# No arithmetic on GpSimd, and a residual summed by accumulating DMAs

## The chip, the cores and the metric

The kernel runs on one core of one Trainium2 chip. The metric is the device time of one execution in microseconds (us). The core's engines run side by side, each through its own queue in order, and wait for each other by semaphores: TensorE (PE in the profile; its weight loads are PEld), VectorE (DVE), ScalarE (ACT), GpSimd (POOL) and SyncE (SP), which only issues DMAs.

## The reference

One sequence of 512 positions with 1024 features goes through two parts, all in float32.

The first part is two layers. Each projects x into three kinds of attention (six heads dilated, four differential, six latent) and joins them; then, with alpha = 4 to the power of 1/4:

```python
h = layer_norm(DEEPNORM_ALPHA * x + heads @ w_o, ln1_g, ln1_b)
ffn = (jax.nn.silu(h @ w_gate) * (h @ w_up)) @ w_down
return layer_norm(DEEPNORM_ALPHA * h + ffn, ln2_g, ln2_b)
```

The second part is one block with modulation vectors (from `w_mod`): a feed-forward part over the sequence and over 256 context positions; then a mixer: retention in both directions over four heads, a convolution of 31 taps over each channel with a layer norm behind it, and two gates:

```python
return (jax.nn.sigmoid(ga) * y_ret + jax.nn.sigmoid(gb) * y_conv) @ w_o
```

and a last feed-forward part with an RMS norm.

## The kernel before

All tensors lie transposed: a tile is 128 features by 512 positions, eight of them (m = 0 to 7) make one state. Every matrix product is taken in three: a float32 operand is split into a high part in the rounded format that TensorE reads, and a low part that is the rest, and high·high, high·low and low·high are summed in PSUM (`mm3`, lines 141 to 145).

**Weights.** `wload` (line 111) loads 512 KB `raw` by SyncE, ScalarE casts it to `whi` (line 109), and `wlo = raw - whi` is a subtraction (line 110) on VectorE or on GpSimd, as `self.wpool` says: it is (0,) (VectorE) nearly everywhere, (1,) for the 16 gate weights of the mixer, and (1, 0), every other one on GpSimd, from there to the mixer's end. Three buffers hold split weights; `hold(2)` adds two.

**Stage ends.** The output projection, the feed-forward parts and the mixer make eight output tiles. The first three go over all 512 positions; the other five (`HELD`) first over positions 0 to 255 for all five, then over 256 to 511, so that the norm of the first half runs on the other engines while TensorE does the second. `ln_add` collects, per tile, the sum `accd` (line 202) and with `sq_add` the sum of squares `accq` (line 216); `ln_first` (line 183) takes K, the feature mean of the first tile, from that tile, and the other tiles get K taken off too. In the feed-forward ends of the two layers these sums run on GpSimd for m below 7 (`"pool": "dq"`, and `"q"` for the RMS norm after the second). `ln_stats` makes mean and variance with TensorE and a short chain of tiny VectorE instructions; `ln_apply` and `affine` write the normed tile as high (`uh`) and low (`ul`) part, and every third low part is taken by GpSimd (line 270).

**Output projection.** `out_chunk` (line 435) multiplies `w_o` with the heads `H` and adds the PSUM result to `D[m]`. `D[m]` is prepared before by two VectorE instructions: `rt` = alpha·xh − K and `D` = alpha·xl + `rt`, where xh and xl are the high and low part of x. PSUM has three buffers `mm` for such products; a buffer is free once the addition has read it.

**Attention.** Eight units in the order `UNITS` = a0 a1 c0 c1 b0 c2 b1 a2; the projections of later units are filled in between the softmax work of earlier ones, so x is read by TensorE until the last unit's projections are done. GpSimd starts DMAs here: the bias tables `T` and the stacked operands `st`.

**Mixer.** `conv_step` hands out taps (line 1147, one `cz` per tap) a few at a time between projections; what is left runs at the end. Then the transposed retention output is normed and gated (`gtd`, line 1262), written to DRAM and read back; `gates` computes 16 gate tiles, nine before and seven after the layer norm statistics of the convolution.

The order on each engine is made by a planner: it takes instructions in program order as priority, and starts each when its inputs are ready by its own estimate of times. So an instruction can stand ahead of one that was written earlier.

Of the kernel before, what the change touches and what calls it, by code (L numbers as in the profile page):

```python
# [9 lines left out]
F32 = mybir.dt.float32  # L10
# [52 lines left out]
class Kern:  # L63
    def __init__(self, ctx, tc, a, o):
# [21 lines left out]
        self.whx = None  # L86
        self.nw = 0

        self.wpool = (0,)
        self.turn = 0  # L90
# [15 lines left out]

    def split(self, src, hi, lo, pool=False):
        nc = self.nc
        nc.scalar.copy(hi, src)  # L109
        (nc.gpsimd if pool else nc.vector).tensor_tensor(out=lo, in0=src, in1=hi.bitcast(F32), op=ALU.subtract)  # L110

    def wload(self, src, key=None):
        if key in self.pre:
            return self.pre.pop(key)
        n = src.shape[-1]
        raw = self.wraw.tile([128, 1024], F32, tag="raw", name="raw")[:, :n]
        self.nc.sync.dma_start(out=raw, in_=src)
        p = self.whl
        if self.whx is not None:
            if self.turn % (3 + self.nx) >= 3:  # L120
                p = self.whx
            self.turn += 1
        hi = p.tile([128, 1024], F32R, tag="hi", name="whi")[:, :n]
        lo = p.tile([128, 1024], F32R, tag="lo", name="wlo")[:, :n]
        self.nw += 1
        self.split(raw, hi, lo, self.wpool[self.nw % len(self.wpool)])
        return hi, lo
# [64 lines left out]
    def ln_add(self, st, m, D, sl=FULL):  # L192
        nc, tmp = self.nc, self.tmp
        if m == 0:
            self.ln_first(st, D)
            st["D0"] = D
        self.sq_add(st, m, D, self.tmp, sl)
        if m == 1:
            st["accd"] = tmp.tile([128, 512], F32, tag="accd", name="accd", bufs=1)
        if m > 0:  # L200
            e = nc.gpsimd if m < 7 and "d" in st.get("pool", "") else nc.vector
            e.tensor_tensor(out=st["accd"][:, sl], in0=(st["D0"] if m == 1 else st["accd"])[:, sl], in1=D[:, sl], op=ALU.add)

    def sq_add(self, st, m, D, p, sl=FULL):
        nc = self.nc
        n = D.shape[-1]
        sl = slice(sl.start, min(sl.stop, n))
        sq = p.tile([128, n], F32, tag="sq", name="sq", bufs=2)
        nc.scalar.activation(out=sq[:, sl], in_=D[:, sl], func=AF.Square)
        if m == 0:  # L210
            st["sq0"] = sq
        else:
            if "accq" not in st:
                st["accq"] = p.tile([128, n], F32, tag="accq", name="accq", bufs=1)
            e = nc.gpsimd if m < 7 and "q" in st.get("pool", "") else nc.vector
            e.tensor_tensor(out=st["accq"][:, sl], in0=(st["sq0"] if m == 1 else st["accq"])[:, sl], in1=sq[:, sl], op=ALU.add)

# [42 lines left out]
    def affine(self, t, g, b, y, x, func=AF.Identity, sl=FULL):  # L260
        nc = self.nc
        nc.scalar.activation(out=y, in_=t, func=func, scale=g, bias=b)
        if x is not None:
# [5 lines left out]
            self.nlo += 1  # L269
            (nc.vector if self.nlo % 3 else nc.gpsimd).tensor_tensor(out=lo, in0=y, in1=hi.bitcast(F32), op=ALU.subtract)  # L270

# [137 lines left out]
    def layer(self, l, X):  # L409
# [5 lines left out]
        with ExitStack() as st:  # L415
            pool = lambda name, bufs: st.enter_context(tc.tile_pool(reuse_waits=RW, name=f"{name}{l}", bufs=bufs))
            self.kq, self.lat, self.pp, self.pt, self.T = pool("kq", 2), pool("lat", 1), pool("pp", 3), pool("pt", 2), pool("T", 2)
            self.tables(self.lat)
            self.wpool = (0,)
            self.attention(l, X, H, lam_init, hp)  # L420
# [9 lines left out]
        stt = {}  # L430
        self.wpool = (0,)
        order = (0, 5, 1, 6, 3, 7, 4, 2)
        stt3 = nc.vector.scalar_tensor_tensor

        def out_chunk(m, sl):
            ps = self.ps_mm.tile([128, 512], F32, tag="mm", name="mm")[:, sl]
            self.chunk(ps, W[m], H, order=order, sl=sl)
            nc.vector.tensor_tensor(out=D[m][:, sl], in0=D[m][:, sl], in1=ps, op=ALU.add)
            self.ln_add(stt, m, D[m], sl)

        for m in range(8):
            xh, xl = (t.bitcast(F32) for t in X[m])
            t = self.tmp.tile([128, 512], F32, tag="t", name="rt")
            if m > 0:
                stt3(out=t, in0=xh, scalar=ALPHA, in1=stt["K"], op0=ALU.mult, op1=ALU.subtract)
            else:
                nc.vector.tensor_scalar(out=t, in0=xh, scalar1=ALPHA, scalar2=None, op0=ALU.mult)
            D.append(accp.tile([128, 512], F32, tag=f"h{m}", name=f"D{m}"))
            stt3(out=D[m], in0=xl, scalar=ALPHA, in1=t, op0=ALU.mult, op1=ALU.add)
            W.append(self.wload(a["w_o"][l, m]))  # L450
            if m < 8 - HELD:
                out_chunk(m, FULL)
# [11 lines left out]

        self.wpool = (0,)
        with ExitStack() as st:
# [4 lines left out]
            acc = [accp.tile([128, 512], F32, tag=f"h{m}", name=f"acc{m}") for m in range(8)]  # L471
            stt = {"pool": "dq"}

# [22 lines left out]
            U = []  # L496
            st2 = {"pool": "q"}

# [121 lines left out]
    def attention(self, l, X, H, lam_init, hp):  # L620
# [237 lines left out]
        for n in range(2 * len(units) + 1):  # L858
            i, hh = n // 2, n % 2
            head = None  # L860
            if i < len(units):
                if hh == 0:
# [3 lines left out]
                    while len(ready) <= i:  # L866
                        step()
                    unit = i
                    maps, *rest = att[units[i][0]](units[i][1], *ready[i])
# [117 lines left out]
    def block2(self, h, X):  # L987
# [46 lines left out]
        st3 = {}  # L1034
        self.wpool = (0,)

# [253 lines left out]
    def mix_out(self, U, h, g2, stt2, tail):  # L1290
        nc, a, tc, tmp = self.nc, self.a, self.tc, self.tmp
        with ExitStack() as st:
# [9 lines left out]

            self.wpool = (1,)
            gates(0, GATES_FIRST)
# [11 lines left out]
            gates(GATES_FIRST, 16)  # L1316
            self.wpool = (1, 0)
            Y = self.mod_tiles()
# [189 lines left out]
```

## Time and profile before

| | |
|---|---|
| time, median of 3 runs | 3099.66 us (3099.3 to 3102.32) |
| profiled execution | 3099.42 us |
| its span, first to last instruction | 3097.6 us |
| mean granted TensorE clock | 0.991 of 2.4 GHz |
| TensorE busy | 3024.2 us (98%) |
| VectorE busy | 1880.2 us (61%), 3552 instructions |
| ScalarE busy | 1158.2 us (37%) |
| GpSimd busy | 275.2 us (9%), 318 instructions |

Busy time is time in which an engine executes. An engine that isn't busy waits, and the profile names what ended the wait, the releaser. The granted clock is given in parts of 2.4 GHz, so 0.50 is 1.2 GHz.

### The profile page before, as it was taken

The page shows a single profiled execution, that of the slowest core. Times are in us where ns is not written, and L with a number is a line of the kernel's source. Part 1 is how long each engine was busy: PE and PEld are TensorE (multiplying, and loading weights), DVE is VectorE, ACT ScalarE, POOL GpSimd, SP SyncE. Part 2 cuts the span into 40 slices and gives each one's busy share as a digit, 9 for nine tenths or more (in the row PEclk, how much of TensorE's full clock was granted, in tenths as well). Part 3 has the DMA queues.
Part 4 walks back from the last instruction along what each step waited for, and adds up shares of the span by engine and source line. Part 5 has one row for each costly group of instructions (what it writes and reads, how often), then busy time and mean ns, then how long its engine had stood idle before and what let it go on. Part 6 is the DMA issues. An engine that isn't in the chain of part 4 may idle for free.

```text
span 3097.6 us, 40929 instructions
## 1 busy us (share of the span) xinstructions
PE 3024.2 (98%) x15961; PEld 2566.7 (83%) x15961; DVE 1880.2 (61%) x3552; ACT 1158.2 (37%) x1908; POOL 275.2 (9%) x318
## 2 busy tenths in 40 slices
PE   9998999999999999999999999999999999999998
PEld 6778888887779888898888888988888778888887
DVE  5988657576888554473323238587887555553334
ACT  4874322245765222262121227433223253342222
POOL 0110000030210000130000001100000343100000
PEclk9999999999999999999999999999999999999999
DMA  4332445322323554322212125623223324233331
GB/s 136 86 86 82 163 136 191 127 85 75 99 85 109 163 170 132 100 93 86 74 53 70 55 69 191 212 83 119 99 92 99 112 86 153 93 103 95 95 94 63
DMA packets 103649, 334.07 MB, mean 108 GB/s; under 512 B 13164, under 2 KB 16364, under 8 KB 103328
## 3 DMA queue, kind: packets, MB, share of 16 engines
q1 hardware_dynamic: 89232, 289.83, 29.5%
q0 software_dynamic: 13136, 40.59, 4.3%
q8 instruction: 125, 2.05, 0.3%
q10 hardware_dynamic: 1088, 1.05, 0.1%
q14 instruction: 68, 0.56, 0.1%
HBM read 312.51 MB, written 14.71 MB: 106 GB/s over the span
## 4 chain that ended last, share of the span: by engine, by line
PE 73%; issue 14%; DVE 7%; ACT 5%; POOL 1%; DMA 1%; POOLq 0%; SPq 0%; DVEq 0%; ACTq 0%
PE mm L143 20%; PE mm L144 20%; PE mm L145 20%; DVE cz L1147 1%; PE gc L145 1%; PE gc L143 1%; PE gc L144 1%; PE pvps L374 1%; ACT P L330 1%; DVE wlo L110 1%; ACT whi L109 1%; PE tps L358 1%; PE dc L145 1%; PE dc L144 1%; PE dc L143 1%
## 5 line engine op out<-in xcount | busy, mean ns | idle before, releaser
L109 ACT CAST whi<-raw 128x1024 fp32r<-128x1024 f32 (+3 forms) x524 | 505.7, 966 | 1402.3 <-PE mm L144 1160.5
L144 PE MATMUL mm<-ul,whi 128*128 128x512 f32 (+2 forms) x2288 | 864.3, 379 | 2.2 <-POOL ul L270 1.7
L143 PE MATMUL mm<-uh,whi 128*128 128x512 f32 (+2 forms) x2288 | 862.9, 380 | 0.8 <-ACT cl L644 0.3
L145 PE MATMUL mm<-uh,wlo 128*128 128x512 f32 (+2 forms) x2288 | 861.9, 378 | 0.3 <-DVE wlo L110 0.2
L110 DVE TENSOR_TENSOR wlo<-raw,whi 128x1024 fp32r<-128x1024 f32 (+3 forms) x484 | 549.4, 1136 | 388.1 <-ACT whi L109 378.7
L144 PEld LDWEIGHTS mm<-ul,whi 128*128 128x128 f32 (+1 forms) x2288 | 431.9, 189 | 82.7 <-POOL ul L270 3.3
L145 PEld LDWEIGHTS mm<-uh,wlo 128*128 128x128 f32 (+1 forms) x2288 | 431.4, 189 | 82.1 <-DVE wlo L110 0.8
L143 PEld LDWEIGHTS mm<-uh,whi 128*128 128x128 f32 (+1 forms) x2288 | 429.8, 189 | 81.0 <-ACT uh L266 1.3
L143 PE MATMUL mm<-hh,whi 128*128 128x512 f32 (+1 forms) x789 | 292.6, 371 | 1.4 <-DVE acc L482 0.7
L144 PE MATMUL mm<-hl,whi 128*128 128x512 f32 (+1 forms) x789 | 292.3, 370 | 0.0
L145 PE MATMUL mm<-hh,wlo 128*128 128x512 f32 (+1 forms) x789 | 291.7, 370 | 0.3 <-DVE wlo L110 0.3
L527 DVE TENSOR_TENSOR g<-g,mm 128x512 f32<-128x512 f32 (+1 forms) x96 | 61.7, 643 | 277.1 <-PE mm L145 273.7
L1147 DVE SCALAR_TENSOR_TENSOR cz<-cy,vec,cz 128x512 f32<-128x512 f32 x240 | 179.2, 773 | 2.2
L143 PEld LDWEIGHTS mm<-hh,whi 128*128 128x128 f32 x789 | 150.3, 191 | 27.0 <-issue 1.1
L145 PEld LDWEIGHTS mm<-hh,wlo 128*128 128x128 f32 x789 | 150.0, 190 | 26.7 <-DVE wlo L110 0.7
L144 PEld LDWEIGHTS mm<-hl,whi 128*128 128x128 f32 x789 | 150.1, 190 | 24.7 <-issue 0.2
L985 DVE SCALAR_TENSOR_TENSOR acc<-mm,g,acc 128x512 f32<-128x512 f32 (+1 forms) x61 | 43.1, 707 | 146.8 <-PE mm L145 146.7
L110 POOL TENSOR_TENSOR wlo<-raw,whi 128x1024 fp32r<-128x1024 f32 (+1 forms) x40 | 88.8, 2221 | 205.5 <-ACT whi L109 204.2
L145 PE MATMUL gc<-uch,wlo 128*128 128x256 f32 x352 | 98.8, 281 | 0.2 <-DVE wlo L110 0.2
L143 PE MATMUL gc<-uch,whi 128*128 128x256 f32 x352 | 98.6, 280 | 0.0
L144 PE MATMUL gc<-ucl,whi 128*128 128x256 f32 x352 | 98.4, 280 | 0.0
L330 ACT ACTIVATE P<-P,nm 128x128 f32<-128x128 f32 (+3 forms) x160 | 88.1, 553 | 20.9 <-DVE nm L326 20.5
(397 smaller groups left out, 4970.7 us busy)
## 6 DMA issues: line engine op xcount, KB each, us to landing
mr<-w_mod SPq DMA_DIRECT2D x72, 512.0 KB, 3.7
raw<-w_f1i SPq DMA_DIRECT2D x54, 512.0 KB, 3.5
raw<-w_gate SPq DMA_DIRECT2D x44, 512.0 KB, 3.6
raw<-w_up SPq DMA_DIRECT2D x44, 512.0 KB, 3.5
raw<-w_f2i SPq DMA_DIRECT2D x44, 512.0 KB, 3.5
raw<-w_in SPq DMA_DIRECT2D x36, 512.0 KB, 3.8
raw<-w_v SPq DMA_DIRECT2D x32, 512.0 KB, 4.0
raw<-w_qk SPq DMA_DIRECT2D x24, 512.0 KB, 3.5
```

The costliest lines, as they stand in the source:

```text
L109: nc.scalar.copy(hi, src)
L110: (nc.gpsimd if pool else nc.vector).tensor_tensor(out=lo, in0=src, in1=hi.bitcast(F32), op=ALU.subtract)
L143: mm(out=ps, lhsT=w[0], rhs=x[0], start=first, stop=False)
L144: mm(out=ps, lhsT=w[0], rhs=x[1], start=False, stop=False)
L145: self.last_mm = mm(out=ps, lhsT=w[1], rhs=x[0], start=False, stop=last)
L330: nc.scalar.activation(out=sl, in_=sl, func=AF.Exp, scale=scale, bias=nm[:, qb:qb + 1], accum_out=sm[:, qb:qb + 1])
L358: nc.tensor.transpose(out=ps[:, w:w + 128], in_=Pt[:, OFF[qb] + kb * 128:OFF[qb] + kb * 128 + 128], identity=self.ident)
L374: nc.tensor.matmul(out=out[:, kb * 128:512], lhsT=v, rhs=blocks[kb][part], start=i == 0, stop=i == 7)
L527: gm = nc.vector.tensor_tensor(out=g, in0=g, in1=pu, op=ALU.mult)
L985: self.nc.vector.scalar_tensor_tensor(out=h, in0=ps, scalar=g[:, m:m + 1], in1=h, op0=ALU.mult, op1=ALU.add)
L1147: nc.vector.scalar_tensor_tensor(out=z, in0=y[:, t:t + 512], scalar=w, in1=z, op0=ALU.mult, op1=ALU.add)
```

## The change

It has two parts.

First, every subtraction and sum that ran on GpSimd runs on VectorE: the weight splits of the mixer, the sums `accd` and `accq`, and the low parts in `affine`. GpSimd then only issues DMAs (and sets up a few constants at the start).

Second, in the output projection. When the last attention unit (number 7) begins in the program, eight DMAs on GpSimd's queue add xh onto xl in place, so that the tile xl holds x. `rt` and the old `D` are gone; `out_chunk` makes `D` = alpha·x + PSUM in one instruction, and for m above 0 takes K off in another.

```diff
-        (nc.gpsimd if pool else nc.vector).tensor_tensor(out=lo, in0=src, in1=hi.bitcast(F32), op=ALU.subtract)
+        nc.vector.tensor_tensor(out=lo, in0=src, in1=hi.bitcast(F32), op=ALU.subtract)
...
-            e = nc.gpsimd if m < 7 and "d" in st.get("pool", "") else nc.vector
-            e.tensor_tensor(out=st["accd"][:, sl], ...
+            nc.vector.tensor_tensor(out=st["accd"][:, sl], ...
...
-            e = nc.gpsimd if m < 7 and "q" in st.get("pool", "") else nc.vector
-            e.tensor_tensor(out=st["accq"][:, sl], ...
+            nc.vector.tensor_tensor(out=st["accq"][:, sl], ...
...
-            (nc.vector if self.nlo % 3 else nc.gpsimd).tensor_tensor(out=lo, in0=y, in1=hi.bitcast(F32), op=ALU.subtract)
+            nc.vector.tensor_tensor(out=lo, in0=y, in1=hi.bitcast(F32), op=ALU.subtract)
...
         def out_chunk(m, sl):
...
-            nc.vector.tensor_tensor(out=D[m][:, sl], in0=D[m][:, sl], in1=ps, op=ALU.add)
+            stt3(out=D[m][:, sl], in0=X[m][1].bitcast(F32)[:, sl], scalar=ALPHA, in1=ps, op0=ALU.mult, op1=ALU.add)
+            if m > 0:
+                nc.vector.tensor_tensor(out=D[m][:, sl], in0=D[m][:, sl], in1=stt["K"][:, sl], op=ALU.subtract)
             self.ln_add(stt, m, D[m], sl)
         for m in range(8):
-            xh, xl = (t.bitcast(F32) for t in X[m])
-            t = self.tmp.tile([128, 512], F32, tag="t", name="rt")
-            if m > 0:
-                stt3(out=t, in0=xh, scalar=ALPHA, in1=stt["K"], op0=ALU.mult, op1=ALU.subtract)
-            else:
-                nc.vector.tensor_scalar(out=t, in0=xh, scalar1=ALPHA, scalar2=None, op0=ALU.mult)
             D.append(accp.tile([128, 512], F32, tag=f"h{m}", name=f"D{m}"))
-            stt3(out=D[m], in0=xl, scalar=ALPHA, in1=t, op0=ALU.mult, op1=ALU.add)
...
+                    if i == 7:
+                        for xh, xl in X:
+                            nc.gpsimd.dma_start(out=xl.bitcast(F32), in_=xh.bitcast(F32), accum_op=ALU.add)
...
-            self.wpool = (1,)
             gates(0, GATES_FIRST)
...
             gates(GATES_FIRST, 16)
-            self.wpool = (1, 0)
```

## Rows read from the trace of the kernel before

**Rows 1.** The page: busy us, share of the span and instructions of each engine.
```profile
PE 3024.2 (98%) x15961; PEld 2566.7 (83%) x15961; DVE 1880.2 (61%) x3552; ACT 1158.2 (37%) x1908; POOL 275.2 (9%) x318
```
**Rows 2.** TensorE's waits: waiting, releaser, us in total, times, longest.
```profile
PE mm L143 <- DVE D L438: 12.2, 4, 4.6
PE gt L1260 <- DVE gtd L1262: 6.5, 1, 6.5
...
PE stps L226 <- DVE accd L202: 5.7, 3, 2.7
```
**Rows 3.** Windows: from:to, length, busy us (instructions) by engine, clock, DMA share.
```profile
core 0: us, PE busy (x) PEld busy (x) DVE busy (x) ACT busy (x) POOL busy (x), PEclk, DMA share, GB/s
248.00:272.00 24.00, 17.10 (x123) 16.65 (x121) 19.58 (x37) 4.83 (x9) 0.00 (x0) 0.86 0.20 66
914.00:938.00 24.00, 18.68 (x130) 18.22 (x128) 22.11 (x44) 7.17 (x16) 0.00 (x0) 0.86 0.22 66
636.00:664.00 28.00, 24.30 (x173) 23.06 (x171) 23.79 (x45) 7.64 (x13) 20.45 (x16) 0.94 0.24 78
1304.00:1328.00 24.00, 21.25 (x144) 19.80 (x143) 17.53 (x39) 6.50 (x11) 13.96 (x14) 0.93 0.18 62
...
2424.00:2446.00 22.00, 15.50 (x67) 12.60 (x66) 20.65 (x24) 3.19 (x5) 9.18 (x9) 0.84 0.39 139
2498.00:2516.00 18.00, 16.00 (x79) 13.14 (x78) 13.15 (x31) 6.76 (x10) 11.91 (x3) 0.91 0.18 59
```
**Rows 4.** VectorE's timeline: start, us, line, operation, tiles, count, [idle before, releaser].
```profile
634.97 1.29 DVE L481 TENSOR_TENSOR acc<-acc,lnk 128x512 f32<-128x512 f32 x2
...
642.33 1.77 DVE L481 TENSOR_TENSOR acc<-acc,lnk 128x512 f32<-128x512 f32 x1
...
653.81 0.93 DVE L202 TENSOR_TENSOR accd<-accd,acc 128x256 f32<-128x256 f32 x1 [2.40 <-POOL accd L202]
...
2397.67 2.72 DVE L1147 SCALAR_TENSOR_TENSOR cz<-cy,vec,cz 128x512 f32<-128x512 f32 x4
...
2423.51 12.88 DVE L1147 SCALAR_TENSOR_TENSOR cz<-cy,vec,cz 128x512 f32<-128x512 f32 x12
```
**Rows 5.** GpSimd's timeline: a table load of the attention, and weight splits.
```profile
208.22 0.55 POOL L306 DMA_DIRECT2D T<-brow  x1 [11.35 <-DVE mx L322]
...
2424.54 2.63 POOL L110 TENSOR_TENSOR wlo<-raw,whi 128x1024 fp32r<-128x1024 f32 x1 [2.60 <-ACT whi L109]
...
2498.74 11.36 POOL L110 TENSOR_TENSOR wlo<-raw,whi 128x1024 fp32r<-128x1024 f32 x2 [6.39 <-ACT whi L109]
```
**Rows 6.** Groups by line and form: busy us, mean ns | idle before, releasers.
```profile
L110 POOL TENSOR_TENSOR wlo<-raw,whi 128x1024 fp32r<-128x1024 f32 x24 | 66.4, 2770 | 158.3 <-ACT whi L109 158.2
...
L270 POOL TENSOR_TENSOR ul<-y,uh 128x256 fp32r<-128x256 f32 x16 | 11.8, 737 | 208.5 <-DVE uh L268 171.1 <-ACT uh L266 34.1 <-issue 3.4
...
L110 DVE TENSOR_TENSOR wlo<-raw,whi 128x1024 fp32r<-128x1024 f32 x366 | 450.1, 1231 | 306.1 <-ACT whi L109 296.6 <-PE mm L145 2.5
```
**Rows 7.** VectorE's timeline in the output projection of layer 0.
```profile
244.32 0.68 DVE L438 TENSOR_TENSOR D<-D,mm 128x512 f32<-128x512 f32 x1
...
249.02 1.29 DVE L445 SCALAR_TENSOR_TENSOR rt<-xh,lnk 128x512 f32<-128x512 f32 x2
...
259.84 1.30 DVE L449 SCALAR_TENSOR_TENSOR D<-xl,rt 128x512 f32<-128x512 f32 x2
...
262.18 0.76 DVE L438 TENSOR_TENSOR D<-D,mm 128x256 f32<-128x256 f32 x2
```
**Rows 8.** Instructions of line 449: ns min/median/max, first and last start.
```profile
L449 DVE SCALAR_TENSOR_TENSOR D<-xl,rt x8: 692/695/696, 238.7 to 260.4; 128x512 f32<-128x512 f32 x8
```
**Rows 9.** Window of the second half of the output projection, layer 0.
```profile
276.00:291.00 15.00, 14.85 (x122) 14.28 (x121) 14.67 (x45) 11.35 (x21) 1.48 (x2) 1.00 0.31 106
```
**Rows 10.** TensorE's timeline: the last product that reads x in layer 0.
```profile
213.53 0.39 PE L145 MATMUL mm<-xh,wlo 128*128 128x512 f32 x1
```
**Rows 11.** DMA issues: queue, count, KB each, median us to landing.
```profile
raw<-w_o SPq DMA_DIRECT2D x16, 512.0 KB, 4.1
...
T<-brow POOLq DMA_DIRECT2D x20, 256.0 KB, 3.6
```

More of the change, by code (lines that the diff above doesn't have):

```diff
@@ L86, in __init__ @@
         self.whx = None
-        self.nw = 0
-        self.wpool = (0,)
         self.turn = 0
@@ L104, in v, with split @@
         return self.vec[:, s:s + 1]
-    def split(self, src, hi, lo, pool=False):
+    def split(self, src, hi, lo):
         nc = self.nc
         nc.scalar.copy(hi, src)
-        (nc.gpsimd if pool else nc.vector).tensor_tensor(out=lo, in0=src, in1=hi.bitcast(F32), op=ALU.subtract)
+        nc.vector.tensor_tensor(out=lo, in0=src, in1=hi.bitcast(F32), op=ALU.subtract)
     def wload(self, src, key=None):
@@ L124, in wload @@
         lo = p.tile([128, 1024], F32R, tag="lo", name="wlo")[:, :n]
-        self.nw += 1
-        self.split(raw, hi, lo, self.wpool[self.nw % len(self.wpool)])
+        self.split(raw, hi, lo)
         return hi, lo
@@ L200, in ln_add @@
         if m > 0:
-            e = nc.gpsimd if m < 7 and "d" in st.get("pool", "") else nc.vector
-            e.tensor_tensor(out=st["accd"][:, sl], in0=(st["D0"] if m == 1 else st["accd"])[:, sl], in1=D[:, sl], op=ALU.add)
+            nc.vector.tensor_tensor(out=st["accd"][:, sl], in0=(st["D0"] if m == 1 else st["accd"])[:, sl], in1=D[:, sl], op=ALU.add)
     def sq_add(self, st, m, D, p, sl=FULL):
@@ L214, in sq_add @@
                 st["accq"] = p.tile([128, n], F32, tag="accq", name="accq", bufs=1)
-            e = nc.gpsimd if m < 7 and "q" in st.get("pool", "") else nc.vector
-            e.tensor_tensor(out=st["accq"][:, sl], in0=(st["sq0"] if m == 1 else st["accq"])[:, sl], in1=sq[:, sl], op=ALU.add)
+            nc.vector.tensor_tensor(out=st["accq"][:, sl], in0=(st["sq0"] if m == 1 else st["accq"])[:, sl], in1=sq[:, sl], op=ALU.add)
     def colsums(self, accs, eps):
@@ L418, in layer @@
             self.tables(self.lat)
-            self.wpool = (0,)
             self.attention(l, X, H, lam_init, hp)
@@ L430, in layer @@
         stt = {}
-        self.wpool = (0,)
         order = (0, 5, 1, 6, 3, 7, 4, 2)
@@ L463, in layer @@
             self.ctx_begin()
-        self.wpool = (0,)
         with ExitStack() as st:
@@ L471, in layer @@
             acc = [accp.tile([128, 512], F32, tag=f"h{m}", name=f"acc{m}") for m in range(8)]
-            stt = {"pool": "dq"}
+            stt = {}
             def down(pi, m, ps, pc, sl):
@@ L496, in layer @@
             U = []
-            st2 = {"pool": "q"}
+            st2 = {}
             def tail1(sl):
@@ L1034, in block2 @@
         st3 = {}
-        self.wpool = (0,)
         def down2(pi, m, ps, pc, sl):
```

## The prediction, made before the changed kernel was run

> **What bounds the kernel now.** I read the page's busy times first [rows 1]: TensorE is busy 98% of the span, VectorE 61%, GpSimd 9%. So the end is set by TensorE, and only two things can move it: time in which TensorE stands still, and time in which its granted clock is at the lower level. Then the list of TensorE's waits [rows 2]: its three largest entries are the places that the edits touch. 12.2 us go to VectorE's addition `D` of the output projection (line 438), 6.5 us to VectorE's `gtd` at the start of the mixer, 5.7 us to `accd`, the sum of the layer norm at the end of the feed-forward parts. Last the windows around these places [rows 3]: each says how long TensorE was idle (length less PE busy) and what clock it had (PEclk; 1.00 is 2.4 GHz, 0.50 is 1.2 GHz). After each stall the clock falls, so a stall costs twice. Idle time, and PE busy times (1 − PEclk):
>
> - output projection, layer 0: 6.9 and 2.4 us; layer 1: 5.3 and 2.6
> - end of the feed-forward part, layer 0: 3.7 and 1.5; layer 1: 2.8 and 1.5
> - start of the mixer: 6.5 and 2.5; its layer norm between the gates: 2.0 and 1.4
>
> That is 39 us, the most that the edits can win here. The reader is to see that VectorE is nearly full in each of these windows (19.6 of 24 us, 22.1 of 24, 20.7 of 22): TensorE waits for VectorE. What counts is whether the edits give VectorE more or less to do just there.
>
> **GpSimd slows VectorE.** The convolution taps show it [rows 4]. Four taps took 2.72 us at 2397, 0.68 each, with GpSimd idle; twelve took 12.88 us at 2423, 1.07 each, while GpSimd split weights (2.63 us the one at 2424) [rows 5]. The subtraction at line 481 takes 1.29 us for a pair at 635, 0.6 each, and 1.77 us alone at 642, under GpSimd's sums [rows 4]. The reverse holds too: two weight splits on GpSimd took 11.36 us together at 2498 [rows 5], against a mean of 2.77 [rows 6]. VectorE does a split in 1.23 us [rows 6], of which about 0.1 overlaps the next. So moving an instruction costs VectorE 1.14 us where it had been losing up to 2.4 us to the same work. Where VectorE was idle, the move costs it time that nobody waits for.
>
> **Output projection.** Removed are `rt` and the old `D` (lines 445 to 449), 8 and 8 per layer, 0.6 us in a row (1.29 for a pair [rows 7]) and 0.69 by itself [rows 8]. In layer 0 fourteen of them, 8.4 us, run between 249.0 and 261.1, and the addition that frees the PSUM buffer for TensorE comes only at 262.18, behind them [rows 7]; that is TensorE's largest stall. Added are subtractions of K: two whole (0.6) and ten half ones (0.33: a pair of half additions takes 0.76 [rows 7]), of which five lie in each half. The fused multiply-add replaces the old addition one for one and doesn't wait for K, so PSUM comes free sooner. In the first half VectorE gets 8.4 − 1.2 − 1.65 = 5.5 us back. What is late next is the second half, where VectorE also applies the layer norm: it is busy 14.67 of 15 us while TensorE, at full clock, is busy 14.85 [rows 9]. There it gets five subtractions (1.65 us) and some two or three of the moved low parts (0.33 each), 2.5 us, and TensorE waits for the last low part of the half. I take the first half's 5.5 us, part of the clock (2.4 us at most), less the 2.5: −4.5 us per layer, −9 for both. Ends: −17.2 (idle and clock all gone) and +5 (nothing won, 2.5 us late twice).
>
> **The accumulating DMAs.** Eight of 256 KB per layer, from GpSimd's queue, after the last read of x by TensorE (213.53 in layer 0 [rows 10]). The first sum is needed by `D` of m = 0, which ran at 244.32, and the last around 262 [rows 7]. Nothing of the attention is queued behind them in GpSimd's queue: its last table load was issued at 208 [rows 5]. No DMA of the trace accumulates. The nearest row is the table load of the same size and queue, 3.6 us to land [rows 11]: one after the other, eight would take 29 us and be there at 242 to 243. Overlapped, they take less; with read and write of the target, up to three times as long, 86 us. I take the row, cost 0, since the first has 31 us and the last 48. Lower end: 0, nothing waited for x before.
>
> **Feed-forward ends.** In the window of layer 0 GpSimd runs 16 sums, 20.5 us, in that of layer 1 14, 14.0 us [rows 3]. On VectorE they cost 0.6 us (whole) and 0.33 (half): 4 × 0.6 + 12 × 0.33 = 6.4 us and 4 × 0.6 + 10 × 0.33 = 5.7. In return the line 481 and the splits lose their stretching (1.77 against 0.6), some 4 us in either, and the 2.40 us that VectorE idled for GpSimd's last sum [rows 4] is time to work in. So VectorE ends about where it did, less that wait. I take −2.5 and −2, half of idle and clock: −4.5. Ends: −9.5 and +12 (no relief at all).
>
> **Mixer start.** 6.5 us of TensorE's wait is for `gtd`, ordered behind twelve taps that took 12.88 us instead of 8.2: 4.7 us late, and 1 or 2 us more on the instructions ahead. The stall is about this lateness. With the change two splits of 1.14 us stand there instead. The time thus falls by 6.2 − 2.3, about 4 us, and with most of the clock's 2.5: −6 us. Ends: −9 and +6 (the rival below).
>
> **Gates and layer norm of the convolution.** Three splits (3.4 us) come onto VectorE while it is full with the layer norm's subtractions and sums; against it stands the end of the two slow GpSimd splits. −1.5 us; ends −3.4 and +3.4. The other splits of the mixer run beside an idle VectorE, cost 0; were that cover gone, some 30 would cost 1.14 each.
>
> **Low parts of the normed tiles.** Two or three per half come from GpSimd (0.74 us [rows 6]) to VectorE (0.33 in a row), in about eight VectorE-paced halves, four outside the output projection: 4 × 2.7 × 0.33 = 3.6 us, against which GpSimd's slowness, a thing TensorE also waited for, ends. +1.5 us; ends 0 and +6.
>
> **Sum.** −9 − 4.5 − 6 − 1.5 + 1.5 = −19.5 us. The profiled execution took 3099.42 us, 1.8 more than its span, and lies 0.2 below the median of 3099.66; I set both equal: 3080 us.
>
> **Rivals.**
> 1. *VectorE becomes the bound (slower).* If GpSimd's work didn't stretch VectorE's as the taps suggest, every moved instruction would be added to a full engine: +12 (feed-forward ends), +3.4 (gates), +6 (low parts), +2.3 (mixer start), less 9 of the output projection, is +15: 3114 us. It decides itself at the feed-forward ends: slower if the added 6.4 and 5.7 us aren't outweighed by the shorter line 481. For it: these windows are full. Against it: 1.77 against 0.6 and 1.07 against 0.68. Chance 0.07.
> 2. *Splits queue behind the taps.* When TensorE comes to the first gate, about 20 taps (13 us at 0.66) and four `gtd` are left on VectorE. If the order puts them ahead of the splits, TensorE waits 6 us more than before instead of 6 less: 3092 us. For it: taps come earlier in the program. Against it: in the trace a split stands between taps wherever it was ready. Chance 0.12.
> 3. *Late sums of x.* At twice the table load's time the eighth sum lands 58 us after 213.5, at 271, 9 us after the need, in both layers: +18, 3098 us. It also covers weights held up: their loads take 4.1 us [rows 11]. Chance 0.08. The Trainium skill (DMA: Bandwidth & Descriptors, Issuing engines are not separate DMA queues) says that transfers started from any engine run on the same 16 DMA engines and interleave, so by it two loads of `w_o` that meet the sums take longer. By that rule, were both 4.1 us loads doubled on TensorE's path in both layers, the time would be 3080 + 16 = 3096. The trace shows a DMA share of 0.20 in that window [rows 3], which leaves room, so it gets no chance beyond the 0.08.
> 4. *More than forecast.* All idle and clock of the six windows gone but for 3 us of new waits: 3063 us. Chance 0.13: it needs an order that fits everywhere.
>
> **How the numbers follow.** The forecast has 0.60: 3080, own range 3068 to 3092. The range runs from 3062, below rival 4, to 3099, above rivals 2 and 3; rival 1 and the tails of 4 are left out. A measurement of this kernel can tell about 0.2%, 6 us, from no change. Faster than 3093.5: 0.60, 0.13, most of rival 2 and a little of 3, 0.83. Same: the rest of 2 and 3, 0.10. Slower: rival 1, 0.07.
>
> **What would show it.** Right: TensorE's waits for `D` (12.2), `gtd` (6.5) and `accd` (5.7) each below a half; taps at 0.66 throughout; line 481 at 0.6; no GpSimd arithmetic; all eight sums landed before `D` of m = 0. Wrong: TensorE waiting for the low part `ul`, for `wlo` at the first gates, or for a DMA on `xl`; the feed-forward windows longer than before.

## The result and the profile after

The changed kernel takes 3068.35 us (median of 4 runs, 3066.45 to 3070.85), the kernel before 3099.48 (median of 4, 3097.11 to 3102.32): a ratio of 0.9900 with a 95% interval of 0.9883 to 0.9917, 31 us less. The forecast was 3080, its own range 3068 to 3092. The sign, the places and the range held; the size came out at the lower edge, 1.6 times the forecast change, and two of the four runs lie below 3068.

The page of the kernel after has this line in place of [rows 1]:

```profile
PE 3012.2 (98%) x15961; PEld 2558.9 (84%) x15961; DVE 1894.4 (62%) x3673; ACT 1159.3 (38%) x1908; POOL 112.9 (4%) x205
```

The span fell from 3097.6 to 3064.4 us, by 33.2. TensorE's busy time fell by 12.0 us with the same 15961 products, which goes with the mean granted clock, 0.994 instead of 0.991. The other 21.2 us are time in which it stood still. VectorE's busy time grew by only 14.2 us, although 129 instructions came over from GpSimd.

TensorE's waits in the kernel after, answering [rows 2]; the columns are the same:

```profile
PE mm L139 <- DVE uh L262: 4.4, 7, 1.5
...
PE stps L220 <- DVE accd L197: 1.6, 2, 1.2
...
PE mm L140 <- DVE ul L264: 1.2, 5, 0.3
...
PE gt L1250 <- DVE gtd L1252: 0.3, 1, 0.3
...
PE mm L139 <- DVE D L431: 0.3, 1, 0.3
```

`D` went from 12.2 to 0.3 us, `gtd` from 6.5 to 0.3, `accd` from 5.7 to 1.6. Two waits for ScalarE now lead the list, 6.8 us for `Ph` in the attention and 6.2 for `xh` at the start; they were there before (6.8 and 6.0), and the change doesn't touch them. Behind them, and new, is `uh`, VectorE's cast of a normed tile, in small pieces.

Windows of the kernel after at the same places as [rows 3], shifted with the program, and two more (from 268 and from 1336); columns as there:

```profile
248.00:272.00 24.00, 23.99 (x203) 23.69 (x202) 21.70 (x59) 7.80 (x14) 0.00 (x0) 1.00 0.32 93
901.00:925.00 24.00, 23.53 (x199) 23.12 (x198) 22.56 (x65) 10.41 (x20) 0.00 (x0) 1.00 0.29 91
268.00:283.00 15.00, 13.52 (x102) 12.19 (x100) 14.69 (x46) 10.51 (x17) 0.00 (x0) 1.00 0.54 176
628.00:656.00 28.00, 27.26 (x213) 26.32 (x211) 26.58 (x72) 9.09 (x16) 0.00 (x0) 1.00 0.29 95
...
1285.00:1309.00 24.00, 24.00 (x184) 22.86 (x183) 22.41 (x60) 8.71 (x15) 0.00 (x0) 1.00 0.26 78
2397.00:2419.00 22.00, 21.68 (x104) 17.82 (x103) 21.86 (x35) 7.12 (x9) 5.25 (x10) 1.00 0.45 153
2469.00:2487.00 18.00, 17.91 (x89) 14.95 (x88) 14.70 (x34) 6.99 (x10) 1.07 (x2) 0.91 0.32 102
...
1336.00:1366.00 30.00, 26.83 (x202) 26.04 (x201) 25.59 (x78) 19.92 (x42) 0.00 (x0) 0.90 0.29 89
```

At the six places of [rows 3] TensorE is now busy for nearly the whole window, in five of them at full clock; at the gates (2469 to 2487) the idle time is gone, but the clock is still 0.91. The other two windows show a price. In the second half of the output projection (268 to 283) VectorE is as full as before [rows 9], and TensorE now stands still for 1.5 us. And from 1336 to 1366, behind layer 1, there is a new stall of 3.2 us with the clock at 0.90; at this place before (1360 to 1390) TensorE was idle for 0.8 us at full clock.

**Where each microsecond went.** Marks that occur once per stage cut the program into stages. The products `kps` of `ln_first` mark the output projections (`D`), the ends of the feed-forward parts (`acc`) and the convolution's norm (`z`); the first start is layer 0's, the last layer 1's. `gc` and `dc` are the context's products, `gh` the gated retention's, `rR` the last norm's. Columns: ns least/median/most, first to last start. First the kernel before:

```profile
L187 PE MATMUL kps<-D,ones x4: 592/592/592, 245.3 to 912.0; 128*128 128x512 f32 x4
L187 PE MATMUL kps<-acc,ones x4: 590/592/697, 632.7 to 1302.1; 128*128 128x512 f32 x4
L187 PE MATMUL kps<-z,ones x2: 592/592/592, 2488.8 to 2489.2; 128*128 128x512 f32 x2
L143 PE MATMUL gc<-uch,whi x352: 276/280/283, 1333.1 to 1844.9; 128*128 128x256 f32 x176
L143 PE MATMUL dc<-hh,whi x176: 277/283/283, 1476.3 to 1864.8; 128*128 128x256 f32 x176
L143 PE MATMUL mm<-gh,whi x128: 387/389/447, 2535.6 to 2624.2; 128*128 128x512 f32 x128
L179 PE MATMUL rR<-ident,rsy x40: 273/275/579, 974.7 to 3090.6; 128*128 128x128 f32 x40
```

And the kernel after:

```profile
L183 PE MATMUL kps<-D,ones x4: 592/592/592, 245.5 to 898.6; 128*128 128x512 f32 x4
L183 PE MATMUL kps<-acc,ones x4: 590/592/697, 624.4 to 1282.5; 128*128 128x512 f32 x4
L183 PE MATMUL kps<-z,ones x2: 592/592/593, 2460.0 to 2460.5; 128*128 128x512 f32 x2
L139 PE MATMUL gc<-uch,whi x352: 276/280/366, 1309.0 to 1824.0; 128*128 128x256 f32 x176
L139 PE MATMUL dc<-hh,whi x176: 277/283/284, 1455.3 to 1843.9; 128*128 128x256 f32 x176
L139 PE MATMUL mm<-gh,whi x128: 389/389/497, 2504.6 to 2592.6; 128*128 128x512 f32 x128
L175 PE MATMUL rR<-ident,rsy x40: 270/275/582, 957.8 to 3057.4; 128*128 128x128 f32 x40
```

The differences of neighbouring marks, us. They come from one profiled execution of each kernel. Over this kernel, the one before and the twelve of the experiments below, the first mark lies between 244.9 and 248.1, so a difference of 2 or 3 us in one stage of one kernel can be chance; one that returns in several kernels is not.

| stage, from mark to mark | before | after | change | forecast |
|---|---|---|---|---|
| start to output projection, layer 0 | 245.3 | 245.5 | +0.2 | 0 |
| output projection, layer 0 (`D` to `acc`) | 387.4 | 378.9 | −8.5 | −4.5 |
| feed-forward end, layer 0 (`acc` to next `D`) | 279.3 | 274.2 | −5.1 | −2.5 |
| output projection, layer 1 | 390.1 | 383.9 | −6.2 | −4.5 |
| feed-forward end, layer 1 (`acc` to `gc`) | 31.0 | 26.5 | −4.5 | −2 |
| context feed-forward (`gc` to `dc`) | 143.2 | 146.3 | +3.1 | 0 |
| to the convolution's norm (`dc` to `z`): mixer start | 1012.5 | 1004.7 | −7.8 | −6 |
| gates (`z` to `gh`) | 46.8 | 44.6 | −2.2 | −1.5 |
| rest (`gh` to the last `rR`) | 555.0 | 552.8 | −2.2 | 0 |
| low parts, spread over the stages | | | | +1.5 |
| sum | | | −33.2 | −19.5 |

VectorE's timeline of the kernel after, answering [rows 4] and [rows 7]; a line of before, for comparison, stands in the next fence:

```profile
261.57 0.42 DVE L431 SCALAR_TENSOR_TENSOR D<-xl,mm 128x256 f32<-128x256 f32 x1 [0.67 <-PE mm L141]
...
635.01 0.68 DVE L468 TENSOR_TENSOR acc<-acc,lnk 128x512 f32<-128x512 f32 x1
...
2399.45 1.93 DVE L1236 TENSOR_SCALAR on<-on,gmv,rsy 128x512 f32<-128x512 f32 x4
2401.28 4.08 DVE L1137 SCALAR_TENSOR_TENSOR cz<-cy,vec,cz 128x512 f32<-128x512 f32 x6
2405.25 1.24 DVE L107 TENSOR_TENSOR wlo<-raw,whi 128x1024 fp32r<-128x1024 f32 x1
```

```profile
2419.57 4.02 DVE L1246 TENSOR_SCALAR on<-on,gmv,rsy 128x512 f32<-128x512 f32 x4
```

At 261.57 VectorE waits for TensorE, where at 262.18 TensorE waited for VectorE [rows 7]. A tap takes 0.68 us again (4.08 for six), the subtraction that was line 481 takes 0.68 alone (0.6 in a row) instead of 1.77, four normings `on` take 1.93 instead of 4.02, and a split stands between the taps.

### The profile page after: what moved, and what is told of

Its sections match the earlier page's. It is cut to its first block, busy times and chain, and to the rows that moved or that the text cites. A ratio compares the mean times of both kernels' runs of the same rounds, so it can differ in the third digit from the quotient of the medians.

```text
span 3064.4 us, 40854 instructions
## 1 busy us (share of the span) xinstructions
PE 3012.2 (98%) x15961; PEld 2558.9 (84%) x15961; DVE 1894.4 (62%) x3673; ACT 1159.3 (38%) x1908; POOL 112.9 (4%) x205
## 4 chain that ended last, share of the span: by engine, by line
PE 87%; DVE 5%; issue 4%; ACT 4%; DMA 0%; POOL 0%; SPq 0%; DVEq 0%; ACTq 0%; POOLq 0%
PE mm L139 25%; PE mm L140 25%; PE mm L141 25%; PE gc L141 1%; PE gc L139 1%; PE gc L140 1%; PE pvps L368 1%; DVE cz L1137 1%; ACT P L324 1%; PE tps L352 1%; ACT whi L106 1%; PE dc L141 1%; PE dc L140 1%; PE dc L139 1%; DVE wlo L107 1%
## 5 line engine op out<-in xcount | busy, mean ns | idle before, releaser
L107 DVE TENSOR_TENSOR wlo<-raw,whi 128x1024 fp32r<-128x1024 f32 (+3 forms) x524 | 584.5, 1117 | 415.3 <-ACT whi L106 401.9
L902 DVE CUSTOM_DVE_ANT_0 mr<-mr,srow,vec 128x1024 f32<-128x1024 f32 x72 | 92.0, 1278 | 1.1 <-ACT srow L893 1.1
```

Of the source, the lines that this page charges most:

```text
L107: nc.vector.tensor_tensor(out=lo, in0=src, in1=hi.bitcast(F32), op=ALU.subtract)
L902: nc.vector.tensor_tensor_reduce(out=raw if i == len(rows) - 1 else junk, in0=raw, in1=rows[i], scale=1.0, scalar=self.vec[:, b0 + j:b0 + ...
```

## The experiments

All are timed against the kernel before; medians, with the 95% interval of the ratio. Differences from the changed kernel are between medians of different rounds, in which the kernel before took 3099.5 to 3100.8 us. The theory is: GpSimd's arithmetic slowed VectorE where TensorE waited for VectorE, and the new residual takes VectorE's work out of the way of the PSUM buffers. The rivals doubt either half: that GpSimd was only late with its own results, and that in the output projection the order counts and not the amount of work.

**e4: GpSimd works for nobody.** The changed kernel, with twelve additions into a tile that nobody reads.

```diff
                     gates.append(sg)
...
+                    if hd == 3:
+                        for _ in range(3):
+                            nc.gpsimd.tensor_tensor(out=self.junk, in0=self.junk, in1=sg, op=ALU.add)
```

> The changed kernel with twelve additions of 128x512 on GpSimd at the start of the mixer, into a tile that nobody reads; nobody waits for them but GpSimd's own later DMA issues. Theory (GpSimd's arithmetic slows VectorE's instructions with two operands in SBUF): the taps beside them go from 0.66 to about 1.07 us, on becomes 1.0 instead of 0.48 us, TensorE waits for gtd again, and the time rises by 4 to 8 us, to 3072 to 3076. Rival (what cost time before was that GpSimd handed its results over late): taps stay at 0.66, time unchanged at 3068 within 2 us.

It took 3080.03 us (0.9936, 0.9923 to 0.9948), 11.7 more than the changed kernel. TensorE's waits:

```profile
PE gt L1252 <- DVE gtd L1254: 8.6, 1, 8.6
```

GpSimd's timeline, and VectorE's beside it:

```profile
2395.94 10.68 POOL L1265 TENSOR_TENSOR junk<-junk,sg 128x512 f32<-128x512 f32 x6 [68.47 <-ACT sg L1261]
...
2412.46 9.27 POOL L1265 TENSOR_TENSOR junk<-junk,sg 128x512 f32<-128x512 f32 x5
...
2423.81 1.28 POOL L1265 TENSOR_TENSOR junk<-junk,sg 128x512 f32<-128x512 f32 x1
```

```profile
2396.22 1.25 DVE L162 TENSOR_TENSOR rst<-rst,rsx 128x4 f32<-128x4 f32 x1
...
2408.20 4.05 DVE L1139 SCALAR_TENSOR_TENSOR cz<-cy,vec,cz 128x512 f32<-128x512 f32 x6
...
2417.20 5.08 DVE L1139 SCALAR_TENSOR_TENSOR cz<-cy,vec,cz 128x512 f32<-128x512 f32 x3
...
2423.53 2.13 DVE L1139 SCALAR_TENSOR_TENSOR cz<-cy,vec,cz 128x512 f32<-128x512 f32 x1
```

At the mixer's start the rival falls: nobody used GpSimd's results, and yet the time went up, by more than expected. Nor is it GpSimd's own DMA issues, now queued behind the additions: TensorE waits for VectorE's `gtd`, and the first of these runs at 2422.21, 11.8 us later than in the changed kernel. The reader is to see that the two engines take turns. An addition takes 1.28 us when it goes through at once (2423.81, while the tap of 2423.53 takes 2.13 instead of 0.68) and 1.78 to 1.85 in a row beside VectorE. An instruction of a norm's chain on 4 columns, 0.16 us elsewhere, takes 1.25 beside an addition. Three taps take 5.08 us, 1.69 each, and at 2408, with GpSimd idle, 0.68. So each GpSimd addition takes about 1.0 us from VectorE, where VectorE would do the same addition in 0.6 itself. The Trainium skill (SBUF — State Buffer, section Who interferes with whom) says that a VectorE instruction with two inputs in SBUF contends with a GpSimd instruction that reads SBUF, and that the pair of ports which the two share is an exclusive lock; the trace agrees with its 1.69 us for a tap instead of 0.68.

**e1 and e2: the two parts by themselves.** e1 is the changed kernel with the old `rt`, `D` and addition and without the accumulating DMAs; e2 is the kernel before with the new `out_chunk` and the DMAs.

```diff
 e1, from the changed kernel
...
-            stt3(out=D[m][:, sl], in0=X[m][1].bitcast(F32)[:, sl], scalar=ALPHA, in1=ps, op0=ALU.mult, op1=ALU.add)
+            nc.vector.tensor_tensor(out=D[m][:, sl], in0=D[m][:, sl], in1=ps, op=ALU.add)
...
 e2, from the kernel before
...
+                            nc.gpsimd.dma_start(out=xl.bitcast(F32), in_=xh.bitcast(F32), accum_op=ALU.add)
```

> The first part alone: GpSimd computes nothing, the residual of the output projection is built as before (rt, then D, ahead of the product), no accumulating DMAs. Theory (the two parts touch different places and add up): the output projection loses again what it won, 8.5 us in layer 0 and 6.2 in layer 1 by the shifts of TensorE's first products, so 3068.4 + 14.7 = 3083 us, and TensorE's wait for D is back at some 12 us. Rival (the parts overlap, since a stall that one takes away lets the other's show): nearer 3075 or 3090.

> The second part alone: accumulating DMAs and fused addition in the output projection, GpSimd's sums, weight splits and low parts as before. Theory (adding up): 3099.5 - 14.7 = 3085 us; the waits for gtd (6.5) and accd (5.7) stay. Rival (in the output projection the low parts on GpSimd were part of the stall): 3088 or more.

e1 took 3081.09 us (0.9935, 0.9921 to 0.9948), e2 3096.01 (0.9985, 0.9976 to 0.9994). The first is as expected (3083), the second is not (3085): 19.7 and 4.8 us less than before make 24.5, and both together take off 31. By the marks, e2's output projections are shorter by 8.0 and only 2.2 us. The next fence has these marks of e2, and TensorE's largest wait in e1 follows:

```profile
L187 PE MATMUL kps<-D,ones x4: 592/592/592, 245.6 to 905.1; 128*128 128x512 f32 x4
L187 PE MATMUL kps<-acc,ones x4: 590/592/697, 625.0 to 1293.0; 128*128 128x512 f32 x4
```

```profile
PE mm L139 <- DVE D L431: 13.8, 4, 4.6
```

e1's two output projections are as long as before to 1 us (+0.1, −0.8): nearly none of the 14.7 us there comes from the first part alone. e2 also lost 5.0 us between `dc` and `z`. From 1888.2 to 1968.2, where the context's projections begin, TensorE is idle for 7.8 us, 2.8 more than at the same place before (2.58 of the 7.8 in a wait for ScalarE's `whi` that ends at 1909.4), and in the 20 us from 1908.2 its clock is 0.83 where it was 1.00, some 3 us. Why that wait arises there isn't shown.

**e3: the order without the saving.** `D` reads PSUM first, then gets the low part in an instruction of its own; the accumulating DMAs are gone (not shown).

```diff
-            stt3(out=D[m][:, sl], in0=X[m][1].bitcast(F32)[:, sl], scalar=ALPHA, in1=ps, op0=ALU.mult, op1=ALU.add)
+            for i in range(2):
+                stt3(out=D[m][:, sl], in0=X[m][i].bitcast(F32)[:, sl], scalar=ALPHA, in1=(ps, D[m][:, sl])[i], op0=ALU.mult, op1=ALU.add)
```

> As the changed kernel, but without the accumulating DMAs: D = alpha xh + psum, then D = D + alpha xl, then D = D - K. VectorE has one instruction more for each piece, 2 whole and 10 half ones a layer for 4.5 us, so that it works about as long here as with rt and the old D; only the order is the new one, the read of psum first and waiting for nothing but TensorE. Theory (the stall came from the order: fourteen instructions queued ahead of the addition that frees psum): most of the 14.7 us stay won; the first half hides its extra 2.9 us, the second half is full and pays 1.65 us a layer, some clock with it: 3068.4 + 3 to 6 = 3072 to 3074 us. Rival (it came from the number of VectorE's instructions): 3068.4 + 9 or more, 3077 to 3083 us.

It took 3077.78 us (0.9928, 0.9916 to 0.9941), 9.4 above the changed kernel: the rival's number. By the marks its output projections gained 2.4 and 2.5 us, of 8.5 and 6.2. Its windows in layer 0, first half and second, columns as in [rows 3]:

```profile
249.00:272.00 23.00, 22.41 (x190) 22.23 (x189) 21.78 (x57) 7.14 (x13) 0.00 (x0) 1.00 0.28 93
...
272.00:292.00 20.00, 15.78 (x113) 13.98 (x111) 18.96 (x54) 11.93 (x20) 0.00 (x0) 0.98 0.43 134
```

Both were half right. In the first half the order alone takes the stall: 0.6 us idle at full clock, where 6.9 us and a clock of 0.86 stood [rows 3]. But the work that is still there moves into the second half, where VectorE has no room (18.96 of 20 us busy), and TensorE stands still for 4.2 us.

**e7, e9, e10: the low parts.** 37 low parts are made by GpSimd before. e7 is the changed kernel with them back on GpSimd; e9 is e2 with them on VectorE; e10 is the kernel before with them on VectorE.

```diff
 e7, from the changed kernel; e9 and e10 the other way
-            nc.vector.tensor_tensor(out=lo, in0=y, in1=hi.bitcast(F32), op=ALU.subtract)
+            (nc.vector if self.nlo % 3 else nc.gpsimd).tensor_tensor(out=lo, in0=y, in1=hi.bitcast(F32), op=ALU.subtract)
```

> The changed kernel with every third low part of the normed tiles back on GpSimd, all else as changed. Theory (a GpSimd instruction costs VectorE about its own length, 0.74 us, where VectorE needs 0.33 to 0.42 for it): slower by 2 to 4 us, 3070 to 3072 us, in the second halves of the output projection and behind the feed-forward parts. Rival (the prediction's own term, the move costs 1.5 us): faster by 1.5 us, 3067 us.

> The kernel before with the new residual and with all low parts of the normed tiles on VectorE; sums and weight splits stay on GpSimd. The residual alone took 4.8 us off the kernel before, and taking the low parts out of the changed kernel cost 6.2. Theory (what the residual wins in the first half of the output projection is lost again in the second as long as GpSimd makes low parts there): 3096 - 6 to 8 = 3088 to 3090 us, layer 1's output projection shorter by 5 to 6 us than before, not by 1.8. Rival (the low parts' 6 us hang on the other moves): 3094 to 3097 us.

> The kernel before with all low parts on VectorE and nothing else changed. Theory (with rt and the old D ahead, the second half starts late and its low parts come out of VectorE's time either way; the low parts pay only where TensorE arrives early): within 2 us of before, 3098 to 3101 us. Rival (GpSimd's low parts always cost VectorE more than its own): 3092 to 3095 us. The prediction's term: 3101 us.

e7 took 3074.62 us (0.9913, 0.9900 to 0.9927), 6.3 more than the changed kernel, though the two intervals overlap. e9 took 3083.48 (0.9941, 0.9928 to 0.9955), 12.5 less than e2, clear of e2's interval. e10 took 3096.26 (0.9981, 0.9973 to 0.9990), 4.4 less than before, between theory and rival; its profiled run (3098.7) was the slowest of its eleven and shows 0.7 us by the marks, so it doesn't settle the size. In it layer 1's output projection is no shorter than before (391.1 us for 390.1). The marks of layer 1's output projection (the last starts) agree between the other two: e7, then e9.

```profile
L183 PE MATMUL kps<-D,ones x4: 592/592/592, 245.9 to 901.2; 128*128 128x512 f32 x4
L183 PE MATMUL kps<-acc,ones x4: 590/592/697, 625.3 to 1289.0; 128*128 128x512 f32 x4
```

```profile
L187 PE MATMUL kps<-D,ones x4: 592/592/592, 245.9 to 905.2; 128*128 128x512 f32 x4
L187 PE MATMUL kps<-acc,ones x4: 590/592/697, 625.7 to 1289.3; 128*128 128x512 f32 x4
```

With low parts on GpSimd the stage takes 387.8 (e7) and 387.9 us (e2), without 384.1 (e9) and 383.9 (the changed kernel): 3.9 us, twice; in the other six kernels with the new residual and its DMAs and no such low parts (e4, e5, e6, e8, e11, e12) it takes 382.3 to 384.2. So this is where the two parts of the change hang together. The next fence shows where the 3.9 us lie, the second half of the stage in e7 and then in the changed kernel, columns as in [rows 3]:

```profile
931.20:951.20 20.00, 17.67 (x96) 16.06 (x95) 15.74 (x57) 8.87 (x16) 1.46 (x2) 0.74 0.41 132
```

```profile
928.60:948.60 20.00, 18.56 (x132) 17.15 (x131) 17.10 (x64) 9.30 (x16) 0.00 (x0) 0.91 0.40 132
```

TensorE idles only 0.9 us longer in e7, but its clock is 0.74 instead of 0.91 there, about 3 us. The residual brings TensorE early to this half, and the low parts make it wait a little more; most of the price is the clock that falls behind the wait. Part of the wait is for GpSimd's own results: e7's list has 2.0 us for `ul` from GpSimd, the changed kernel's has none. Behind `gh` the low parts show as well: 554.5 to 555.0 us with them on GpSimd (e7, e2, before), 552.7 to 552.9 without (e9, e10, the changed kernel). By e7's other marks 1.7 us each go at the end of layer 0 and on the way to the convolution's norm, and 1.5 come in at the context's stage; these are within what equal code differs by.

**e5, e6, e12: the sums and the splits.** e5 puts the sums `accd` and `accq` back on GpSimd, e6 the mixer's splits, e12 only the sums of squares for the norm behind layer 1. The lines that read these settings are put back with them (not shown).

```diff
 e5
-            stt = {}
+            stt = {"pool": "dq"}
...
-            st2 = {}
+            st2 = {"pool": "q"}
 e6
+            self.wpool = (1,)
             gates(0, GATES_FIRST)
...
             gates(GATES_FIRST, 16)
+            self.wpool = (1, 0)
 e12
-            st2 = {}
+            st2 = {"pool": "q"}
```

> The changed kernel with the sums of the layer norms at the ends of the feed-forward parts back on GpSimd, and layer 1's sum of squares for the next norm too. Theory (GpSimd's additions cost VectorE more than VectorE's own would, and come late): the end in layer 0 loses its 5.0 us again and that of layer 1 4.5, while the 3.1 us that the changed kernel gives back between 1309 and 1455 come in again: 3068.4 + 6.4 = 3075 us. Rival (these ends won nothing of their own, the shift there came from low parts): 3068 to 3070 us.

> The changed kernel with the mixer's weight splits back on GpSimd (all of the first gates, every second one after them). Theory: the mixer's start loses 8.6 us again and the gates 2.9, TensorE's wait for gtd is back at 6 to 7 us: 3068.4 + 11 = 3079 to 3080 us. Rival (the start of the mixer came earlier because of what was ahead of it): 3068 to 3072 us.

> The changed kernel with only the sums of squares for the norm behind layer 1 back on GpSimd, seven half-tile additions in either half, where the changed kernel gave back 3.1 us between 1309 and 1455. Theory (that was the last half's chain of sums on a full VectorE, 25.6 of 30 us): the 3 us come in again, 3065 us. Rival (GpSimd's additions cost VectorE their own length there as well, 0.7 us each against 0.33): 3069 to 3072 us.

e5 took 3072.37 us (0.9907, 0.9893 to 0.9920), e6 3079.70 (0.9930, 0.9918 to 0.9943), e12 3062.85 (0.9879, 0.9865 to 0.9892). By the marks e5 loses 6.4 us at the end of layer 0 and 4.6 at that of layer 1, and gains 4.1 in the context's stage: the theory's places, though the median moved by 4.0 only and the intervals of e5 and the changed kernel overlap. The places return in the other kernels: the end of layer 1 takes 31.0 to 32.0 us in the five with these sums on GpSimd (before, e2, e5, e9, e10) and 26.5 or 26.6 in the nine with them on VectorE. Here the sums' lateness and their slowing of VectorE act together [rows 4], and e5 doesn't part them. e6 loses 7.2 at the mixer's start and 2.8 at the gates, its median 11.3, and TensorE waits for `gtd` as in [rows 2]:

```profile
PE gt L1254 <- DVE gtd L1256: 6.5, 1, 6.5
```

Behind `gh`, where e6 has every second split on GpSimd, it loses 0.1 us: there VectorE has time to spare. e12's context stage takes 142.8 us instead of 146.3 (its twelve additions are six in either half, not seven), and in the window around it, columns as in [rows 3], TensorE has its clock again:

```profile
1311.20:1368.00 56.80, 54.44 (x440) 52.41 (x439) 49.42 (x146) 41.44 (x84) 10.05 (x12) 1.00 0.34 109
```

At the same place (1309 to 1366) the changed kernel has 4.7 us of idle time instead of 2.4 and a clock of 0.95. All six kernels with these sums on GpSimd take 140.8 to 143.2 us for the stage, the eight others 144.0 to 146.5. So the 3.1 us that the change gave back come from these sums on a full VectorE; for twelve additions GpSimd is the cheaper place here. Whether e12 as a whole beats the changed kernel isn't settled: the intervals overlap, and e11 below, which does more than the changed kernel, came to 3063.75.

**e8: high parts on ScalarE.**

```diff
-            if self.nlo % 2:
-                nc.scalar.activation(out=hi, in_=t, func=func, scale=g, bias=b)
-            else:
-                nc.vector.tensor_copy(hi, y)
+            nc.scalar.activation(out=hi, in_=t, func=func, scale=g, bias=b)
```

> The changed kernel with the high parts of the normed tiles all written by ScalarE, where VectorE casts every second one now; TensorE waits 4.4 us in seven places for such a cast. Theory (what is left of these stalls is VectorE's throughput): most of the 4.4 us go and some of the waits for ul and accd: 3063 to 3066 us. Rival (ScalarE, 10.5 of 15 us busy in the second half of the output projection, with twice the y and high parts becomes what TensorE waits for): 3069 to 3074 us, with TensorE waiting for uh of ScalarE.

It took 3078.47 us (0.9926, 0.9913 to 0.9938). The waits for VectorE's `uh` went; in their place stand these:

```profile
PE mm L139 <- ACT whi L106: 13.2, 4, 7.0
...
PE mm L139 <- ACT uh L259: 4.2, 5, 1.6
```

The rival held, beyond its own 3074: TensorE waits 4.2 us for `uh` of ScalarE, as it said, and more, by another way, for ScalarE's cast of weights, 7.0 us of it from 1892 on, where the context's projections begin. What VectorE is relieved of there falls on an engine that is needed just as soon.

**e11: the sums of x twice.** The second round adds the high part once more, so this kernel computes something else; the other instructions are the same.

```diff
-                        for xh, xl in X:
+                        for xh, xl in X + X:
                             nc.gpsimd.dma_start(out=xl.bitcast(F32), in_=xh.bitcast(F32), accum_op=ALU.add)
```

> The changed kernel with the eight accumulating DMAs of each layer done twice, one round behind the other, so that x's high part is added twice. One round has landed by about 230 in layer 0, and D of m = 0 needs its sum at 244.5. Theory (the sums have some 15 us to spare): the second round lands at about 245 to 250, tiles 0 and 1 may wait a few us, the rest not: 3068 to 3074 us. Rival (late sums are near already): each layer waits 10 us or more, 3088 us and up, with VectorE's D waiting for a DMA.

It took 3063.75 us (0.9883, 0.9870 to 0.9897): the second round costs nothing that can be measured in the time. In its profiled execution, the slowest of the four at 3068.40, layer 0's output projection is 2.4 us longer than in the changed kernel without more idle time: in the 20 us from 275.9 TensorE is idle for 1.2 us and the clock is 0.83, where in the changed kernel's (from 275.5) it is idle for 1.6 us at 1.00. So the clock doesn't fall alike behind like stalls. The last of the second round's issues on GpSimd's queue:

```profile
229.34 0.87 POOL L858 DMA_DIRECT2D xl<-xh  x1 [0.41 <-DMA xl<-xh]
```

In the changed kernel one round is issued from 208.63 to 216.4. The next two fences have its DMAs in layer 0: the loads of `w_o` from 200 to 245 (KB each, median us to landing), and the landing of the eight that write `xl`:

```profile
raw<-w_o SPq DMA_DIRECT2D x5, 512.0 KB, 8.7
```

```profile
DMA to landing us min/median/max: 3.4/12.7/15.5
```

The slowest took 15.5 us, so all have landed by 232, and the first is needed at 244.5. The loads of `w_o` take 8.7 us beside them instead of 4.1 [rows 11], which agrees with the Trainium skill's rule in rival 3 (DMA: Bandwidth & Descriptors, Issuing engines are not separate DMA queues: transfers started from any engine run on the same 16 DMA engines). But TensorE doesn't wait for them: from 208 to 248 it is idle for 0.1 us.

## Why the prediction was right, and where its sizes were off

**The bound and the places: right.** Of the 33.2 us won, 34.3 lie in the six stages whose windows offered 39 of idle time and clock, and 2.2 behind `gh`, outside these windows; 3.1 went back. The prediction calls the waits for `D`, `gtd` and `accd` the three largest of the list, which is not so: 6.8 us for `Ph` and 6.0 for `xh` stand between them. Nothing hangs on that, since the edits don't touch those two. All the signs that were to show it right are there: the three waits fell below a half, taps and the old line 481 are at their short length, all sums landed before `D` of m = 0. Of the signs against it, TensorE's waits for `ul` come to 1.2 us; for `wlo` at the first gates and for the sums of x it does not wait.

**Output projection: −14.7 us for a forecast of −9, the largest miss.** The first half was mis-sized. The prediction took VectorE's saved time, 5.5 us, and part of the clock. In fact the whole stall and the whole clock went, 6.9 and 2.4 us in layer 0. e3 shows why: the stall's length was not VectorE's surplus of work but the queue ahead of the addition. With PSUM read first 0.6 us of it are left, though VectorE is as full as ever in that half (21.78 of 23 us). The second half was called late by 2.5 us; in layer 0 it is late by 1.5 at full clock, in layer 1 by 1.4 with the clock at 0.91.

**Low parts: +1.5 forecast, −4.4 to −12.5 measured (e10 alone, e7 −6.3, e9 beside the residual), the one wrong sign.** The price put on them was VectorE's own 0.33 us each, and GpSimd's slowness was only named. e4's rows are of larger instructions; by them most of GpSimd's 0.74 us each is taken out of VectorE too, while it is full, which for low parts is an estimate. What the prediction left out is the clock behind the wait (e7): 3.9 us, mostly clock, sit in layer 1's output projection and so in the −14.7 above, and about 2 are the −2.2 behind `gh`.

**Feed-forward ends: −9.6 for −4.5, less 3.1 given back.** "Half of idle and clock" was too careful: the stretched line 481 and the 2.40 us in which VectorE idled for GpSimd's last sum [rows 4] went, and the −9.6 are as much as both windows had (9.5). What is late next was looked for in the same windows only; it stood 30 us further on, in the norm behind layer 1, where the moved sums of squares meet a full VectorE (e5, e12). So here a term of +3 was missing.

**Mixer: −7.8 and −2.2 for −6 and −1.5.** The taps' lateness was the cause, as e4 and e6 show from both sides. The "1 or 2 us more on the instructions ahead" are the four `on`, 4.02 us before and 1.93 after, 2.1 us. With them the first `gtd` runs 4.9 us earlier, counted from the `dc` mark, for a forecast of about 4; the rest of the 7.8 is about the clock's share (2.5). At the gates the idle time went (2.0 to 0.1 us), and the clock did not come back (0.91 in both).

**The DMAs: 0, right**, with more to spare than shown (e11). They overlapped: one takes 12.7 us at the median instead of the table load's 3.6, but all eight have landed within 24 us of the first issue. One assumption failed without harm: a table load of the attention is issued behind three of them, at 210.54, and lands after 9.4 us.

**Rivals.** VectorE is not the bound: the 129 moved instructions, 70 us by VectorE's own lengths (24 splits at 1.14, 16 half ones and 14 whole sums or low parts at 0.6, 75 half tiles at 0.33), raised its busy time by only 24.5 us in e1; the difference, some 46 us, is the stretching that went. Splits did not queue behind taps. Sums were not late. "More than forecast" at 3063 was 5 us off the result, the forecast 12: the truth lies between, nearer to it.

## What to carry to other kernels

GpSimd's arithmetic is not free help where TensorE waits for a full VectorE: in e4 each addition of 1.28 us took about 1.0 from VectorE. Where VectorE has time to spare it costs nothing (e6 behind `gh`: 0.1 us for every second split). e12 shows an exception, so try the place rather than go by the rule alone. When the instruction that reads PSUM, and so frees its buffer, stands behind others that need no product, put it first, and only then look at how much work is left, since that lands in the next stretch. And add up parts of a change with care: what one part wins can be held back by the next thing in line until another part moves it. Last, a stall of one more microsecond can cost three more in clock (e7), and the clock doesn't fall alike behind like stalls (e11).

## What was not expected of the hardware

- GpSimd and VectorE alternate by whole instructions: a VectorE instruction on 4 columns took 1.25 us instead of 0.16 beside GpSimd additions of 128x512 (e4), and a tap of 128x512 1.69 instead of 0.68.
- An instruction with one tile and two columns as inputs is held up too: four `on` took 4.02 us beside a GpSimd split and 1.93 without.
- An accumulating DMA of 256 KB from SBUF to SBUF landed in 12.7 us (3.4 to 15.5) with eight under way, against 3.6 for a plain table load of that size, and slowed 512 KB loads from 4.1 to 8.7 us, at a DMA share of 0.79 in that stretch (208 to 232; 0.24 before).
